# The up projection of a feed-forward layer: additions queued per part as the last passes are issued, pair loads placed further ahead, prepared sums in a buffer of their own

## The chip, the core and the metric

The kernel runs on one core of a Trainium2 chip. The metric is device time in microseconds (us) of one execution, median of several runs. TensorE does the matrix products (PE in the profile), VectorE (DVE) and ScalarE (ACT) prepare operands and move results, GpSimd (POOL) and SyncE (SP) here mostly issue transfers.

## What is computed

One decoder layer on 256 tokens of width 2048, all in float32: an RMSNorm, a joint input projection, two attention branches of 8 heads each, an output projection with residual, and a feed-forward part. The change is in the feed-forward part alone:

```python
h = _rmsnorm(x, norm_mlp_pre[layer])
u = jnp.square(jax.nn.relu(h @ w_up[layer]))      # w_up: 2048 x 8192
x = x + _rmsnorm(u @ w_down[layer], norm_mlp_post[layer])
```

## The kernel before

**Products.** Every float32 operand is split in two parts, `hi` (the rounded value) and `lo` (the remainder), and a product is three matmuls: hi\*hi, lo\*hi, hi\*lo. A weight tile is 128 rows x 1024 columns. ScalarE makes its `hi` (L306; L310 where a gain is multiplied in), then VectorE its `lo` (L307, L311). There are 8 buffers for split tiles (`W_BUFS`), so a split can be at most 8 tiles ahead of TensorE, and the program queues the splits 6 tiles ahead (`W_AHEAD`). Raw weights come through 5 `raw` buffers, loaded from SyncE's queue.

**Chunks.** `h @ w_up` is done in 8 chunks (`j`) of 1024 columns over 16 row blocks. The result of a chunk has four parts `(b, n)`: two halves of the tokens, two halves of the columns, each one PSUM bank (`acc`). The table `UP_STEPS` gives the steps of a chunk. `k8` is one row block: 12 matmuls. `w1` is a pair of row blocks (2 and 3) done with seven block products where eight would be needed (21 matmuls, four weight tiles): both raw blocks are loaded into the one buffer `ab` from GpSimd's queue (`load_two`), VectorE forms their sums `t` and `u` (L359, L363, L364; 2.6 us together in the trace), and four tiles are split: b11, b, u, t. `p0` is such a pair whose sums were made in DRAM earlier in the kernel (`prepare`), by transfers that add; its four tiles are loaded through `raw` buffers from SyncE's queue. Chunks 1 to 5 have the steps `k8 k9 k10 k11 p0 k12 w1 k13 w2 p3 k14 k15`, chunks 6 and 7 have three `w` pairs and no `p`.

**End of a chunk.** The seven products need four more PSUM banks (`m`). After a chunk's last pair, `close` turns them into four tiles `c` (L1052 on ScalarE, four L1055 on VectorE). Each part of the chunk is then finished by `up_evac`: VectorE adds `c` to the part (L954), ScalarE applies Relu (`r`, L957), TensorE transposes the result (`rt`, four small matmuls, L300), ScalarE squares it into `uT` (L971). These `rt` steps stand in TensorE's queue among the matmuls of the next chunk.

**Order.** Every engine takes its instructions in the order in which the program queued them. That order comes from `Flow`, a planning clock that advances by an assumed cost for every matmul; `up_evac` is a generator whose `yield` values say how long after one step the next is queued. In the kernel before, all four `up_evac` chains start at the end of the chunk, each with a delay of `UP_STEP * (o + 0.1)` ahead of its addition, `UP_STEP` = 2.2. `weights.first[i]` holds work that is queued just ahead of tile number `i`; `plan_seven` puts the sums of a `w` pair two tiles (`SUMS_AHEAD`) ahead of its first tile.

Tiles are numbered through the whole program. Chunk 1 begins with tile 137, chunk 2 with 161, chunk 3 with 185, chunk 4 with 209, chunk 5 with 233, chunk 6 with 257, chunk 7 with 279; the down projection `u @ w_down` begins with tile 301.

Of the kernel before, what the change touches and what calls it, by code (L numbers as in the profile page):

```python
# [18 lines left out]
F32 = mybir.dt.float32  # L19
# [4 lines left out]
OP = mybir.AluOpType  # L24
PSUM = bass.MemoryType.PSUM

P = 128
# [18 lines left out]
CW = 1024  # L46
# [46 lines left out]
D_UP, UP_STEP = 1.8, 2.2  # L93


SUMS_AHEAD = 2
NUP = FF // CW


def steps_of(text):  # L100

    return [(s[0], int(s[1:])) for s in text.split()]


UP_STEPS = {0: [("k", k) for k in range(KD)]}
for _j in range(1, 6):
    UP_STEPS[_j] = steps_of("k8 k9 k10 k11 p0 k12 w1 k13 w2 p3 k14 k15")
for _j in range(6, NUP):
    UP_STEPS[_j] = steps_of("k6 k7 k8 k9 k10 w0 k11 k12 w1 k13 w2 k14 k15")
SCALED = {j: range(8) for j in range(1, NUP)}  # L110
# [56 lines left out]
class Weights:  # L167
# [15 lines left out]
    def load(self, src, w, name, queue=None):  # L183
        raw = self.pool.tile([P, CW], F32, tag="raw", bufs=RAW_BUFS, name=name)
        out = raw[:, :w]
        if len(src.shape) == 3:
            out = out.rearrange("p (k n) -> p k n", k=src.shape[1])
        (queue or self.nc.sync).dma_start(out=out, in_=src)
        return raw
# [74 lines left out]
def layer(nc, tc, io):  # L264
    flow = Flow()
# [37 lines left out]
    def split(hi, lo, src, g=None):  # L303
        if g is not None:
            return split_gain(hi, lo, src, g)
        nc.scalar.activation(hi, src, AF.Copy)  # L306
        nc.vector.tensor_tensor(out=lo, in0=src, in1=hi.bitcast(F32), op=OP.subtract)  # L307
# [9 lines left out]
    weights = Weights(nc, wp, split, W_BUFS, W_AHEAD)  # L317
# [23 lines left out]
    def up_weight(j, k):  # L341
        return io["w_up"][k * P:(k + 1) * P, j * CW:(j + 1) * CW]

    late = {}
    sums_kept = {jk: dram.tile([P, 2 * CW], F32, name=f"sums{jk[0]}_{jk[1]}") for jk in PREP}

    def seven(load, targets):

        st, tt, H = {}, nc.vector.tensor_tensor, 512

        def sums():
            ab = load()
            a, b = st["a"], st["b"] = [ab[:, :CW], ab[:, CW:]] if not isinstance(ab, list) else ab
            t, u = st["t"], st["u"] = targets()
            if not isinstance(ab, list):
                two = [x.rearrange("p (k n) -> p k n", n=H) for x in (t, ab)]
                tt(out=two[0], in0=two[1][:, 0:2, :], in1=two[1][:, 1:4:2, :], op=OP.add)  # L359
            else:  # L360
                for x, o in ((a, 0), (b, H)):
                    tt(out=t[:, o:o + H], in0=a[:, o:o + H], in1=x[:, H:], op=OP.add)
            tt(out=u[:, :H], in0=t[:, :H], in1=b[:, H:], op=OP.add)  # L363
            tt(out=u[:, H:], in0=u[:, :H], in1=b[:, :H], op=OP.add)  # L364

        def b11(hi, lo):
            split(hi[:, :H], lo[:, :H], st["a"][:, :H])

        return sums, [b11] + [lambda hi, lo, n=n: split(hi, lo, st[n]) for n in "but"]

    def load_two(raw, queue, src):
        for i in range(2):
# [29 lines left out]
        st, left[c, kp] = down_parts(c, kp)  # L402
        nc.gpsimd.dma_start(out=st.bitcast(F32), in_=skeep[kp])

    def plan_seven(sums, fs, after, more=(), last=()):

        at = max(len(weights.specs) - SUMS_AHEAD, after)
        for n, f in (*more, (0, sums), *((0, f) for f in last)):
            weights.first.setdefault(at - n, []).append(f)
        return [weights.plan(f) for f in fs], len(weights.specs)  # L410

    wide_u, after = [], 0
    for j in range(NUP):
        wide_u.append([])
        for what, k in UP_STEPS[j]:
            if what == "k":
                g = () if k in SCALED.get(j, ()) else (gcol[:, 8 + k:9 + k],)
                ts = [weights.plan(up_weight(j, k), 1, CW, *g)]  # L420
            elif what == "p":
                kept = sums_kept[j, k]
                ts = [weights.plan(src, 1, n) for src, n in (
                    (up_weight(j, 2 * k)[:, :512], 512), (up_weight(j, 2 * k + 1), CW),
                    (kept[:, CW:], CW), (kept[:, :CW], CW))]
            else:
                ts, after = plan_seven(*seven_up(j, k), after)
            wide_u[j].append((what, k, ts))

    def down_weight(c, k):  # L430
# [518 lines left out]

    def up_evac(j, b, i, acc, order, more=None):  # L950

        yield UP_STEP * order
        if more is not None:
            nc.vector.tensor_tensor(out=acc, in0=acc, in1=more, op=OP.add)  # L954
            yield 1.6
        r = late["up"].tile([P, 512], F32, tag="r", bufs=2, name=f"r{j}_{b}")
        nc.scalar.activation(r, acc, AF.Relu, scale=rstd2[b])  # L957
        yield D_UP if j > 1 else 2 * D_UP
        t = bank(i, f"rt{j}_{b}")
        for k in range(4):  # L960
            transpose(t[:, k * P:(k + 1) * P], r[:, k * P:(k + 1) * P])
        if j not in uT:
            if j in (12, 13):
                t2 = late["ab"][:, (j - 12) * CW:(j - 11) * CW]
            elif j == 10:
                t2 = late["up"].tile([P, CW], F32, tag="uT10", bufs=1, name="uT10")
            else:
                tag = {"tag": "T", "bufs": 2} if j > 13 else {}
                t2 = late["up"].tile([P, CW], F32, name=f"uT{j}", **tag)
            uT[j] = t2.rearrange("p (k s) -> p k s", k=4)  # L970
        nc.scalar.activation(uT[j][:, :, b * P:(b + 1) * P], t.rearrange("p (k s) -> p k s", k=4), AF.Square)  # L971
# [53 lines left out]
    def some_sums(kps, after=0.0):  # L1025
        yield after
        for kp in kps:
            yield from left_sums(kp)
# [34 lines left out]
    for j in range(FF // CW):  # L1063
        at = {bn: 4 * (j % 2) + i for i, bn in enumerate(PARTS)}
        if j == 0:
            accs = {bn: acc_bank(f"acc_u0_{bn[0]}{bn[1]}") for bn in at}
            at = {bn: (turn[0] - 3 + i) % 4 for i, bn in enumerate(at)}
        else:
            accs = {bn: bank(i, f"acc_u{j}_{bn[0]}{bn[1]}") for bn, i in at.items()}
        steps = wide_u[j]  # L1070
        order = in_order(len(steps), (APART[1], 0)) if j == 0 else [(t, b) for t, (w, _, _) in enumerate(steps)
                                                                    for b in range(NB if w == "k" else 1)]
        for t, b in order:
            what, k, tiles = steps[t]
            if (j, t, b) == (0, 8, 0):
                flow.finish(*res)
                late["po"].release()
                mix.release()
                late["up"] = pool("up", "right")
                late["st"] = late["up"].tile([P, 3 * CW], F32R, tag="st", bufs=1, name="st")  # L1080
                for n in ("ab", "c"):
                    late[n] = late["up"].tile([P, 2 * CW], F32, name=n)
                late["st2"] = late["up"].tile([P, CW], F32R, tag="uT10", bufs=1, name="st2")
                flow.start(some_sums((0, 1)))
                flow.start(some_sums((2, 3), 18.0))
            if (j, t, b) == (FF // CW - 1, 4, 0):
                weights.limit -= 1
                u_next = split_u(0, 0)
            if what != "k":
                flow.until(lambda: len(sums) > k)  # L1090
            if what == "k":
                w = weights.get(tiles[0])
                h_done(k, b)
                for n in range(2):
                    c = slice(n * 512, (n + 1) * 512)
                    three(accs[b, n], [tok(hT[x], k, b) for x in range(2)], [w[x][:, 0, c] for x in range(2)], t == 0, t == len(steps) - 1)
                    if j == 0 and t == len(steps) - 1:
                        evac.append(flow.start(up_evac(n, b, at[b, n], accs[b, n], 2 * b + n - 0.25 * (2 * b + n))))
                    flow.pump()
                if b == NB - 1:  # L1100
                    weights.free(tiles[0])
                continue

            pairs = [s[1] for s in steps if s[0] != "k"]
            first, last = k == pairs[0], k == pairs[-1]
            if first:
                m = {n: bank(i, f"m{n}_{j}") for n, i in zip((1, 6, 7, 5), free)}
            blocks = [[tok(hT[x], 2 * k + kk, bb) for x in range(2)] for kk, bb in ((0, 0), (1, 0), (1, 1))]
            seven_products(tiles, (blocks, sums[k]), accs, m, first, last)
            if last:  # L1110
                more = close(closing(), m)
        free = [at[bn] for bn in PARTS]
        if j:
            for o, (b, n) in enumerate(PARTS):
                evac.append(flow.start(up_evac(2 * j + n, b, at[b, n], accs[b, n], o + 0.1, more[b, n])))
    u_last = evac[-4:]
    up = late["up"]

# [195 lines left out]
```

## Time and profile before

| | |
|---|---|
| median of 3 runs | 1063.76 us (1063.56 to 1064.2) |
| the profiled execution: its own time | 1066.42 us |
| its span from first to last instruction | 1064.6 us |
| PE busy | 1041.5 us (98%) |
| DVE busy | 811.2 us (76%) |
| ACT busy | 631.1 us (59%) |
| POOL busy | 94.5 us (9%) |
| mean granted TensorE clock | 0.997 |

In the trace chunk 1 begins at 403 us and the down projection at 719.5 us. A row of the timeline has the start, the time from start to end, engine, line, operation, what it writes and reads, the count of merged instructions, and in brackets the idle time ahead of it with what ended it. Matmuls overlap: one is shown 0.39 us long, and the next starts 0.227 us after it.

### The profile page before, as it was taken

The numbers are of one execution on the slowest core, as the hardware profiler recorded it, in microseconds if no ns is written. First come the engines' busy times: TensorE is split into PE (matmuls) and PEld (weight loads), VectorE is DVE, ScalarE is ACT, GpSimd is POOL, SyncE is SP. The second block draws the span as 40 slices with busy tenths as digits, with TensorE's granted clock in tenths as the row PEclk, the third lists the DMA queues.
The fourth block names the chain that finished last, engine by engine and source line by source line (L and its number), as shares of the span: only waits on it lengthen the run. The fifth ranks groups of instructions, "written<-read, shape, count | busy, mean of one in ns | idle before, by whom it ended". The sixth has DMA issues, their size and how long they took to land.

```text
span 1064.6 us, 13618 instructions
## 1 busy us (share of the span) xinstructions
PE 1041.5 (98%) x4839; PEld 863.4 (81%) x4839; DVE 811.2 (76%) x1083; ACT 631.1 (59%) x846; POOL 94.5 (9%) x148
## 2 busy tenths in 40 slices
PE   9999999999999999999999999999999999999996
PEld 6888899888888788777878778888888888888885
DVE  6666546577556678878788798988799978989995
ACT  6574436566454566565665657666566664766761
POOL 0011111112001000000000000001000001122100
PEclk9999999999999999999999999999999999999998
DMA  9999879699887285748676484469688867788952
GB/s 309 350 297 289 212 200 328 201 268 278 236 230 235 95 310 188 254 155 283 201 229 223 160 286 166 157 221 325 233 296 280 279 239 250 283 302 294 372 202 81
DMA packets 94724, 260.81 MB, mean 245 GB/s; under 512 B 8896, under 2 KB 13504, under 8 KB 94272
## 3 DMA queue, kind: packets, MB, share of 16 engines
q1 hardware_dynamic: 74080, 199.00, 54.3%
q0 software_dynamic: 20000, 60.30, 21.0%
q8 instruction: 38, 0.62, 0.2%
q10 hardware_dynamic: 576, 0.64, 0.2%
q14 instruction: 30, 0.25, 0.1%
HBM read 244.18 MB, written 39.32 MB: 266 GB/s over the span
## 4 chain that ended last, share of the span: by engine, by line
PE 72%; DVE 12%; DMA 8%; issue 4%; ACT 3%; DVEq 0%; POOL 0%; POOLq 0%; ACTq 0%; SPq 0%
PE y L296 25%; PE acc_o L296 8%; PE acc_u L296 6%; PE md L296 5%; PE acc_qk L296 4%; DVE lo L307 4%; PE acc_v L296 4%; DMA raw<-in_w_up 4%; PE acc_ckv L296 2%; DVE lo L311 2%; DMA ab<-in_w_up 2%; PE acc_ukv L296 2%; PE acc_q L296 2%; PE acc_cq L296 2%; PE acc_k L296 2%
## 5 line engine op out<-in xcount | busy, mean ns | idle before, releaser
L307 DVE TENSOR_TENSOR lo<-raw,hi 128x1024 fp32r<-128x1024 f32 (+3 forms) x257 | 288.0, 1142 | 96.5 <-ACT hi L306 95.8
L306 ACT ACTIVATE hi<-raw 128x1024 fp32r<-128x1024 f32 (+3 forms) x257 | 250.8, 992 | 101.4 <-PE y L296 20.8
L296 PE MATMUL y<-hi,uhi 128*128 128x512 f32 x376 | 146.6, 390 | 0.0
L296 PE MATMUL y<-hi,ulo 128*128 128x512 f32 x376 | 146.4, 389 | 0.0
L296 PE MATMUL y<-lo,uhi 128*128 128x512 f32 x376 | 146.3, 389 | 0.0
L296 PE MATMUL acc_u<-hi,hT_hi 128*128 128x512 f32 x356 | 142.4, 400 | 3.6 <-DVE c L1055 3.5
L296 PE MATMUL acc_u<-lo,hT_hi 128*128 128x512 f32 x356 | 139.1, 391 | 0.8 <-DVE lo L311 0.8
L296 PE MATMUL acc_u<-hi,hT_lo 128*128 128x512 f32 x356 | 139.2, 391 | 0.4 <-DVE hT_lo L307 0.4
L311 DVE SCALAR_TENSOR_TENSOR lo<-raw,gcol,hi 128x1024 fp32r<-128x1024 f32 x72 | 91.8, 1281 | 27.1 <-ACT hi L310 26.6
L310 ACT ACTIVATE hi<-raw,gcol 128x1024 fp32r<-128x1024 f32 x72 | 82.5, 1149 | 32.8 <-DMA raw<-in_w_up 18.3
L296 PEld LDWEIGHTS y<-lo,uhi 128*128 128x128 f32 x376 | 70.6, 188 | 14.7
L296 PEld LDWEIGHTS y<-hi,ulo 128*128 128x128 f32 x376 | 70.6, 188 | 14.6
L296 PEld LDWEIGHTS y<-hi,uhi 128*128 128x128 f32 x376 | 70.6, 188 | 14.5
L296 PEld LDWEIGHTS acc_u<-hi,hT_hi 128*128 128x128 f32 x356 | 66.9, 188 | 18.8 <-DVE c L1055 6.2
L296 PEld LDWEIGHTS acc_u<-hi,hT_lo 128*128 128x128 f32 x356 | 66.8, 188 | 15.1 <-DVE hT_lo L307 0.8
L296 PEld LDWEIGHTS acc_u<-lo,hT_hi 128*128 128x128 f32 x356 | 67.0, 188 | 14.0 <-DVE lo L311 1.2
L296 PE MATMUL m<-hi,st 128*128 128x512 f32 x156 | 56.5, 389 | 0.0
L296 PE MATMUL acc_o<-hi,mixT_hi 128*128 128x512 f32 x128 | 51.8, 405 | 0.0
L307 DVE TENSOR_TENSOR lo<-st_down,hi 128x1024 fp32r<-128x1024 f32 x40 | 48.0, 1220 | 4.0 <-ACT hi L306 3.8
L296 PE MATMUL acc_o<-hi,mixT_lo 128*128 128x512 f32 x128 | 50.2, 392 | 0.0
L296 PE MATMUL acc_o<-lo,mixT_hi 128*128 128x512 f32 x128 | 50.0, 390 | 0.0
L306 ACT ACTIVATE hi<-st_down 128x1024 fp32r<-128x1024 f32 x40 | 42.1, 1052 | 11.1 <-PE y L296 9.5
(326 smaller groups left out, 2000.8 us busy)
## 6 DMA issues: line engine op xcount, KB each, us to landing
raw<-in_w_down SPq DMA_DIRECT2D x88, 512.0 KB, 5.9
raw<-in_w_up SPq DMA_DIRECT2D x86, 512.0 KB, 5.0
raw<-in_w_in SPq DMA_DIRECT2D x55, 512.0 KB, 6.2
raw<-in_w_out SPq DMA_DIRECT2D x32, 512.0 KB, 7.5
ab<-in_w_up POOLq DMA_DIRECT2D x28, 512.0 KB, 4.9
sums<-in_w_up SPq DMA_DIRECT2D x20, 512.0 KB, 7.2
raw<-sums SPq DMA_DIRECT2D x20, 512.0 KB, 3.9
ab_down<-in_w_down POOLq DMA_DIRECT2D x20, 512.0 KB, 6.7
```

What stands on the lines that cost most here:

```text
L296: nc.tensor.matmul(out, a, b, start=start, stop=stop)
L306: nc.scalar.activation(hi, src, AF.Copy)
L307: nc.vector.tensor_tensor(out=lo, in0=src, in1=hi.bitcast(F32), op=OP.subtract)
L310: nc.scalar.activation(hi, src, AF.Copy, scale=g)
L311: nc.vector.scalar_tensor_tensor(out=lo, in0=src, scalar=g, in1=hi.bitcast(F32), op0=OP.mult, op1=OP.subtract)
```

## The change

1. `up_evac` is started for each part right after the part's last matmuls are issued, and queues the addition 0.2 us later by the planning clock. Relu follows 1.4 us and then `UP_STEP * 0.75 * (2b + n)` later.
2. The load of a `w` pair (`early`) is queued up to `LOAD_AHEAD` = 3 tiles ahead of its sums, in chunks 1 to 6 and for the first pair of chunk 7.
3. In chunks 1 to 4 the prepared sums (t and u of a `p` pair) come in one load of 1 MB into the buffer `tu`, from GpSimd's queue; before, they were two loads of 512 KB through `raw` buffers from SyncE's queue. Chunk 5 keeps the old way.
4. In chunks 1 to 5 the pairs 2 and 3 change roles: `p2` stands between `w1` and `w3`, so the last pair is now `w3`.
5. `uT` tiles 8 and 9 take the place of `tu` once it is no longer needed.

```diff
-SUMS_AHEAD = 2
+SUMS_AHEAD, LOAD_AHEAD = 2, 3
 for _j in range(1, 6):
-    UP_STEPS[_j] = steps_of("k8 k9 k10 k11 p0 k12 w1 k13 w2 p3 k14 k15")
+    UP_STEPS[_j] = steps_of("k8 k9 k10 k11 p0 k12 w1 k13 p2 w3 k14 k15")
...
         def sums():
-            ab = load()
+            ab = st["ab"] if "ab" in st else load()
...
-        return sums, [b11] + [lambda hi, lo, n=n: split(hi, lo, st[n]) for n in "but"]
+        def early():
+            st["ab"] = load()
+
+        return sums, [b11] + [lambda hi, lo, n=n: split(hi, lo, st[n]) for n in "but"], early
...
-    def plan_seven(sums, fs, after, more=(), last=()):
+    def plan_seven(sums, fs, early, after, more=(), last=(), soon=False):
 
         at = max(len(weights.specs) - SUMS_AHEAD, after)
+        if soon:
+            more = (*more, (at - max(at - LOAD_AHEAD, after - 2), early))
...
-                ts = [weights.plan(src, 1, n) for src, n in (
-                    (up_weight(j, 2 * k)[:, :512], 512), (up_weight(j, 2 * k + 1), CW),
-                    (kept[:, CW:], CW), (kept[:, :CW], CW))]
+                srcs = [(up_weight(j, 2 * k)[:, :512], 512), (up_weight(j, 2 * k + 1), CW),
+                        (kept[:, CW:], CW), (kept[:, :CW], CW)]
+                if j < 5:
+                    at = max(len(weights.specs) - 2 * LOAD_AHEAD, after_p)
+                    weights.first.setdefault(at, []).append(
+                        lambda kept=kept: nc.gpsimd.dma_start(out=late["tu"], in_=kept))
+                    ts = [weights.plan(src, 1, n) for src, n in srcs[:2]] + [weights.plan(
+                        lambda hi, lo, o=o: split(hi, lo, late["tu"][:, o:o + CW])) for o in (CW, 0)]
+                    after_p = len(weights.specs)
+                else:
+                    ts = [weights.plan(src, 1, n) for src, n in srcs]
             else:
-                ts, after = plan_seven(*seven_up(j, k), after)
+                ts, after = plan_seven(*seven_up(j, k), after, soon=j < NUP - 1 or k == 0)
...
     def up_evac(j, b, i, acc, order, more=None):
 
+        if more is not None:
+            yield 0.2
+            nc.vector.tensor_tensor(out=acc, in0=acc, in1=more, op=OP.add)
+            yield 1.4
         yield UP_STEP * order
-        if more is not None:
-            nc.vector.tensor_tensor(out=acc, in0=acc, in1=more, op=OP.add)
-            yield 1.6
         r = late["up"].tile([P, 512], F32, tag="r", bufs=2, name=f"r{j}_{b}")
...
+            elif j in (8, 9):
+                if j == 8:
+                    late["uT8"] = late["up"].tile([P, 2 * CW], F32, tag="uT8", bufs=1, name="uT8")
+                t2 = late["uT8"][:, (j - 8) * CW:(j - 7) * CW]
...
+                late["tu"] = late["up"].tile([P, 2 * CW], F32, tag="uT8", bufs=1, name="tu")
...
-                    if j == 0 and t == len(steps) - 1:
-                        evac.append(flow.start(up_evac(n, b, at[b, n], accs[b, n], 2 * b + n - 0.25 * (2 * b + n))))
+                    if t == len(steps) - 1:
+                        evac.append(flow.start(up_evac(2 * j + n, b, at[b, n], accs[b, n], 0.75 * (2 * b + n),
+                                                       more[b, n] if j else None)))
...
-        if j:
-            for o, (b, n) in enumerate(PARTS):
-                evac.append(flow.start(up_evac(2 * j + n, b, at[b, n], accs[b, n], o + 0.1, more[b, n])))
```

VectorE's queue around the end of chunk 2, before. `c` is a tile of `close`, `lo189` a split of weight tile 189, `acc_u2_01` part (0, 1) of chunk 2, `t3_1` and `u3_1` the sums of pair `w1` of chunk 3:

```order
L1055 TENSOR_TENSOR c_3572<-c_3572,m7_2_4242 128x512
L307 TENSOR_TENSOR lo189_4467<-raw189_4464,hi189_4466 128x512
L307 TENSOR_TENSOR lo190_4485<-raw190_4482,hi190_4484 128x1024
L307 TENSOR_TENSOR lo191_4507<-raw191_4504,hi191_4506 128x1024
L954 TENSOR_TENSOR acc_u2_00_4127<-acc_u2_00_4127,c_3572 128x512
L359 TENSOR_TENSOR t3_1_4525<-ab_3571 128x1024
L363 TENSOR_TENSOR u3_1_4526<-t3_1_4525,ab_3571 128x512
L364 TENSOR_TENSOR u3_1_4526<-u3_1_4526,ab_3571 128x512
L307 TENSOR_TENSOR lo192_4533<-raw192_4530,hi192_4532 128x1024
L954 TENSOR_TENSOR acc_u2_01_4128<-acc_u2_01_4128,c_3572 128x512
L954 TENSOR_TENSOR acc_u2_10_4129<-acc_u2_10_4129,c_3572 128x512
L311 SCALAR_TENSOR_TENSOR lo193_4564<-raw193_4561,gcol_69,hi193_4563 128x1024
```

The same place now (L967 is the addition, L1073 the last operation of `close`):

```order
L1073 TENSOR_TENSOR c_3572<-c_3572,m7_2_4241 128x512
L307 TENSOR_TENSOR lo189_4459<-raw189_4456,hi189_4458 128x512
L307 TENSOR_TENSOR lo190_4477<-raw190_4474,hi190_4476 128x1024
L967 TENSOR_TENSOR acc_u2_00_4128<-acc_u2_00_4128,c_3572 128x512
L967 TENSOR_TENSOR acc_u2_01_4129<-acc_u2_01_4129,c_3572 128x512
L967 TENSOR_TENSOR acc_u2_10_4130<-acc_u2_10_4130,c_3572 128x512
L307 TENSOR_TENSOR lo191_4500<-tu_3574,hi191_4499 128x1024
L967 TENSOR_TENSOR acc_u2_11_4131<-acc_u2_11_4131,c_3572 128x512
L359 TENSOR_TENSOR t3_1_4527<-ab_3571 128x1024
L363 TENSOR_TENSOR u3_1_4528<-t3_1_4527,ab_3571 128x512
L364 TENSOR_TENSOR u3_1_4528<-u3_1_4528,ab_3571 128x512
L307 TENSOR_TENSOR lo192_4533<-tu_3574,hi192_4532 128x1024
```

The first addition stands one split earlier, the other three stand ahead of the three sums, and `lo191`, `lo192` read `tu`.

TensorE's queue at the first transposes of chunk 2's result (`rt4_0`), before; tile 186 is the second tile of chunk 3:

```order
L296 MATMUL acc_u3_10_4502<-hi186_4425,hT_lo_2921 128x512
L296 MATMUL acc_u3_11_4503<-hi186_4425,hT_hi_2920 128x512
L296 MATMUL acc_u3_11_4503<-lo186_4426,hT_hi_2920 128x512
L296 MATMUL acc_u3_11_4503<-hi186_4425,hT_lo_2921 128x512
L300 MATMUL rt4_0_4553<-ident_94,r4_0_4539 128x128 x4
L296 MATMUL acc_u3_00_4500<-hi187_4437,hT_hi_2920 128x512
```

And now; tile 185 is the first tile of chunk 3:

```order
L296 MATMUL acc_u3_10_4497<-hi185_4406,hT_lo_2921 128x512
L296 MATMUL acc_u3_11_4498<-hi185_4406,hT_hi_2920 128x512
L296 MATMUL acc_u3_11_4498<-lo185_4407,hT_hi_2920 128x512
L296 MATMUL acc_u3_11_4498<-hi185_4406,hT_lo_2921 128x512
L300 MATMUL rt4_0_4518<-ident_94,r4_0_4507 128x128 x4
L296 MATMUL acc_u3_00_4495<-hi186_4415,hT_hi_2920 128x512
```

The transposes moved 12 matmuls earlier: they stand 12 matmuls into the next chunk, where before they stood 24 in. The other three of each chunk moved 12 earlier as well (21, 30 and 39 instead of 33, 42 and 51), and so at the ends of chunks 1 to 7; those of chunk 0 stay.

GpSimd's queue before, where it enters the up projection:

```order
L504 TENSOR_TENSOR rstd_pre20_3413<-t_pre20_3412,neg_half_92 128x1
L504 TENSOR_TENSOR rstd_pre21_3508<-t_pre21_3507,neg_half_92 128x1
L374 DMA ab_3571<-in_w_up 128x1024 x28
L374 DMA ab_down_6360<-in_w_down 128x1024 x2
L374 DMA c_3572<-in_w_down 128x1024 x2
```

And now:

```order
L517 TENSOR_TENSOR rstd_pre21_3508<-t_pre21_3507,neg_half_92 128x1
L433 DMA tu_3574<-sums1_0_70 128x2048
L377 DMA ab_3571<-in_w_up 128x1024 x2
L433 DMA tu_3574<-sums1_2_71 128x2048
L377 DMA ab_3571<-in_w_up 128x1024 x2
L433 DMA tu_3574<-sums2_0_72 128x2048
L377 DMA ab_3571<-in_w_up 128x1024 x2
```

Eight loads of `tu` now stand between the pair loads, in chunks 1 to 4.

More of the change, by code (lines that the diff above doesn't have):

```diff
@@ L410, in plan_seven @@
         return [weights.plan(f) for f in fs], len(weights.specs)
-    wide_u, after = [], 0
+    wide_u, after, after_p = [], 0, 0
     for j in range(NUP):
```

## The prediction

> **What bounds the kernel now.** I read the page's table of engines first, then busy time by stage, then what TensorE waits for, then the timelines around those waits.
>
> ```profile
> PE 1041.5 (98%) x4839; PEld 863.4 (81%) x4839; DVE 811.2 (76%) x1083; ACT 631.1 (59%) x846; POOL 94.5 (9%) x148
> 403.00:719.50 316.50, 304.33 (x1379) 247.03 (x1378) 263.36 (x286) 197.54 (x231) 13.97 (x26) 1.00 0.64 211
> 719.50:1047.00 327.50, 327.50 (x1454) 271.24 (x1453) 285.24 (x325) 201.65 (x224) 33.28 (x62) 1.00 0.78 272
> ```
>
> The stage rows give the length, then busy time of PE, weight loads, DVE, ACT, POOL, and the granted clock (1.00). TensorE is the bound: it is idle for 23.1 us of the 1064.6. Half of that, 12.2 us, lies in chunks 1 to 7 of the up projection (403 to 719.5); the down projection behind it has none. So the change can win only by taking TensorE's waits out of chunks 1 to 7. All of them there:
>
> ```profile
> PE rt L300 <- ACT r L957: 7.7, 6, 1.6
> PE acc_u L296 <- DVE c L1055: 3.5, 3, 1.3
> PE acc_u L296 <- DVE lo L311: 0.8, 1, 0.8
> ```
>
> Ten waits, 12.0 us: six of transposes on Relu (ends of chunks 1 to 4), three of a chunk's first matmuls on `close` (one when chunk 2 begins, two when chunk 6 begins), one on a late split (chunk 1). A wait costs more than is recorded for it. One that waited, and one that didn't:
>
> ```profile
> 457.03 0.40 PE L296 MATMUL acc_u<-hi,hT_lo 128*128 128x512 f32 x1
> 459.00 0.66 PE L300 MATMUL rt<-ident,r 128*128 128x128 f32 x4 [1.58 <-ACT r L957]
> 459.42 0.47 PE L296 MATMUL acc_u<-hi,hT_hi 128*128 128x512 f32 x1
> ...
> 463.95 0.40 PE L296 MATMUL m<-hi,hT_lo 128*128 128x512 f32 x1
> 464.19 0.60 PE L300 MATMUL rt<-ident,r 128*128 128x128 f32 x4
> 464.54 0.48 PE L296 MATMUL acc_u<-hi,hT_hi 128*128 128x512 f32 x1
> ```
>
> From matmul to matmul 2.39 us against 0.59: 1.80 lost where 1.58 is recorded, 0.22 more per wait. The ten cost 12.0 + 2.2 = 14.2 us, the most that the change can win.
>
> **Why the transposes wait: the end of chunk 2.** Chunk 3 begins at E = 493.91 (first row).
>
> ```profile
> 493.91 0.39 PE L296 MATMUL acc_u<-hi,hT_hi 128*128 128x512 f32 x1
> ...
> 499.69 0.60 PE L300 MATMUL rt<-ident,r 128*128 128x128 f32 x4
> ...
> 488.60 3.87 DVE L311 SCALAR_TENSOR_TENSOR lo<-raw,gcol,hi 128x1024 fp32r<-128x1024 f32 x3 [0.81 <-ACT hi L310]
> 492.39 2.28 DVE L1055 TENSOR_TENSOR c<-m,c 128x512 f32<-128x512 f32 x3
> 494.70 0.69 DVE L1055 TENSOR_TENSOR c<-c,m 128x512 f32<-128x512 f32 x1
> 495.30 2.95 DVE L307 TENSOR_TENSOR lo<-raw,hi 128x512 fp32r<-128x512 f32 x3
> 498.17 0.69 DVE L954 TENSOR_TENSOR acc_u<-acc_u,c 128x512 f32<-128x512 f32 x1
> 498.77 1.21 DVE L359 TENSOR_TENSOR t<-ab 128x1024 f32<-128x1024 f32 x1
> 501.36 1.22 DVE L307 TENSOR_TENSOR lo<-raw,hi 128x1024 fp32r<-128x1024 f32 x1
> 502.50 1.29 DVE L954 TENSOR_TENSOR acc_u<-acc_u,c 128x512 f32<-128x512 f32 x2
> ...
> 498.90 0.69 ACT L957 ACTIVATE r<-acc_u,rstd_pre 128x512 f32<-128x512 f32 x1 [0.50 <-DVE acc_u L954]
> 503.22 0.69 ACT L957 ACTIVATE r<-acc_u,rstd_pre 128x512 f32<-128x512 f32 x1 [3.63 <-DVE acc_u L954]
> ```
>
> The second addition stands behind three sums and a split, so it begins 4.3 us after the first; its Relu ends at 503.9, where the second transposes wait 1.6 us. The change takes those four operations away from in between. But it also moves all transposes 12 matmuls (12 x 0.227 = 2.72 us) earlier, so the first ones, which did not wait here, now have a deadline. From an addition's start to its transposes takes 499.69 - 498.17 = 1.52 us. The transposes now stand at E + 2.72; so the first addition must begin by E + 1.20.
>
> When can it begin? Ahead of it in VectorE's queue stand the four operations of `close` (492.39 to 495.30, 2.91 us) and now two splits instead of three (2.95 us for three, 1.74 for two). `close` needs the last pair's products, which end two steps before the chunk's end: 24 x 0.227 = 5.44 us. The earliest start is E - 5.44 + 2.91 + 1.74 = E - 0.8, which leaves 2.0 us of slack. Today VectorE comes to `close` at 492.39 = E - 1.5, 3.9 us after the earliest. If it stays that late, the first addition begins at 498.17 less one split (1.13) = 497.04 = E + 3.1, and TensorE waits 1.9 us. What decides is whether VectorE gets 1.9 us earlier per chunk.
>
> **What VectorE gains within a chunk.**
>
> ```profile
> DVE t L359 <- DMA ab<-in_w_up: 14.8, 6, 3.0
> ACT hi L306 <- DMA raw<-sums: 12.2, 8, 2.9
> POOL ab L374 <- DVE lo L307: 267.9, 25, 39.1
> ...
> 446.81 0.39 PE L296 MATMUL acc_u<-hi,hT_hi 128*128 128x512 f32 x1
> 421.04 1.22 DVE L307 TENSOR_TENSOR lo<-t,hi 128x1024 fp32r<-128x1024 f32 x1
> 425.25 1.23 DVE L359 TENSOR_TENSOR t<-ab 128x1024 f32<-128x1024 f32 x1 [3.00 <-DMA ab<-in_w_up]
> ```
>
> (a) *Order of the pairs.* Today `w2` follows `w1` with one tile between, and VectorE waits for `ab`: 14.8 us in six waits, 2.5 each, once in each of chunks 1 to 6. With `p2` between, VectorE has four 1024-column splits and one of 512 (some 5.3 us) between freeing `ab` and the sums, against a load of 4.8 us (row below). Five of the six waits go; chunk 6 keeps its own. Gain 2.5 us per chunk. (b) *Prepared sums in `tu`.* ScalarE's waits on `raw<-sums`, 12.2 us in chunks 1 to 5, mostly go: `tu` is free when the pair before has been split, half a chunk ahead, and the `raw` buffers turn over six times per pair section, not ten, so the six splits at the chunk's end find their weights loaded. Before the last three of them VectorE waits 0.8 us in chunk 2 (row 488.60). (c) *The load-ahead* by itself is worth nothing: GpSimd has nothing else to do there and stands waiting for the split that frees `ab` (267.9 us in 25 waits); the place of the load in the program only sets the turns with `tu`. (d) The additions themselves take no more time, 4 x 0.6 us.
>
> (a) alone is more than the 1.9 us needed, (b) comes on top, and VectorE's work (263 us in this stage, unchanged by the edit) fits the 304 us that TensorE needs. So at the ends of chunks 2, 3 and 4 I expect `close` at its earliest and no wait. Three places remain.
>
> *End of chunk 1.* The gain starts only at 422.2, where the last split before 425.25 ends (row 421.04). From there the new order is split k13 (1.2), p2's two raw splits (1.7), the sums as `ab` lands (425.25 to 427.85, as now), two `tu` splits (2.3), four of w3 (4.0): 434.1. Six more splits at 1.28, the last held until its `raw` buffer is loaded (freed 435.4, some 5.5 us to land, 1.2 on ScalarE), end at 443.4; `close` and two splits make it 448.1. The chunk's end, today at 446.8 (first PE row), comes 1.0 us earlier by the vanished wait on a split: E = 445.8, deadline 447.0. TensorE waits 1.1 us.
>
> *Ends of chunks 5 and 6.* Here VectorE is held by the 8 buffers of split tiles, not by loads. The end of chunk 6:
>
> ```profile
> 666.12 1.06 ACT L306 ACTIVATE hi<-raw 128x1024 fp32r<-128x1024 f32 x1 [1.61 <-PE acc_u L296]
> ...
> 669.55 1.22 DVE L359 TENSOR_TENSOR t<-ab 128x1024 f32<-128x1024 f32 x1
> 672.14 1.27 DVE L311 SCALAR_TENSOR_TENSOR lo<-raw,gcol,hi 128x1024 fp32r<-128x1024 f32 x1
> 676.25 1.28 DVE L311 SCALAR_TENSOR_TENSOR lo<-raw,gcol,hi 128x1024 fp32r<-128x1024 f32 x1
> 677.44 1.82 DVE L307 TENSOR_TENSOR lo<-ab,hi 128x512 fp32r<-128x512 f32 x2
> ...
> 681.56 0.60 PE L300 MATMUL rt<-ident,r 128*128 128x128 f32 x4
> ```
>
> ScalarE waits for TensorE to free a tile at 666.12, and the sums of the next `w0` stand ahead of `close`. E = 681.56 - 5.44 = 676.12. The addition moves ahead of one of the two splits begun at 677.44, so to 678.04 = E + 1.92, 0.72 us past the deadline. No wait today becomes one of 0.72. Chunk 5's end has the same rows in the same order, and once its loads are not late it gets the same 0.72 in place of today's two waits on `close`. At the end of chunk 7 the order has no sums and I find none.
>
> Sum: 14.2 removed; added 1.1 + 0.72 + 0.72, and 3 x 0.22, together 3.2. Net 11.0 us. The traced execution's span becomes 1064.6 - 11.0 = 1053.6; its own time was 1066.4, 2.7 above the median of the runs, so I take the sum off the median: 1063.8 - 11.0 = 1052.8 us.
>
> **Moved loads.** Eight 1 MB loads on GpSimd's queue replace sixteen of 512 KB on SyncE's. The bytes stay.
>
> ```profile
> raw<-in_w_up SPq DMA_DIRECT2D x65, 512.0 KB, 4.8
> ab<-in_w_up POOLq DMA_DIRECT2D x26, 512.0 KB, 4.8
> raw<-sums SPq DMA_DIRECT2D x18, 512.0 KB, 3.9
> xkeep<-x SPq DMA_DIRECT2D x2, 1024.0 KB, 4.9
> ```
>
> A `tu` load has no row. Its time is bounded by the 1 MB transfer (4.9 us) and by two 512 KB loads one after the other (9.6); I take 7. The one for the next chunk's `p0` can start when `p2` is split (430.1 in the working above) and is needed when ScalarE reaches it, about 447: 17 us. Hidden at either end, so it adds nothing to the sum. If it were late, ScalarE would stand at the `tu` split that is queued right ahead of the first Relu, and TensorE behind that.
>
> The Trainium skill speaks against this move: "SBUF — State Buffer", section "SBUF: two separate sides", says that GpSimd cannot write descriptors while VectorE runs an operation in its two-port mode, so that a transfer issued by GpSimd seems blocked, and it advises the SyncE or ScalarE queue. By that rule the load would grow, and the sum with it once the 17 us are used up. This trace shows no such hold: with VectorE busy for 83% of the stage, GpSimd's pair loads land in the same 4.8 us as SyncE's.
>
> **Rivals.** *Nothing left over*: splits at chunks 1, 5 and 6 come 0.7 to 1.1 us sooner than worked out. Against it, the buffer limit at 666.12. 1063.8 - 14.2 = 1049.6. Chance 0.12.
> *Half the gain*: VectorE gets about 1 us less than needed at the ends of chunks 2, 3 and 4, because 1 MB `tu` loads lie beside `ab` and `raw` loads and each lands later. Each boundary keeps about 1 + 0.22: 1052.8 + 3.7 = 1056.5. Chance 0.14.
> *No earlier at all*: the waits only trade places. 1.9 + 0.22 at four ends (8.5), the two waits on `close` at the start of chunk 6 stay (3.5 less some 1.2 for the one in chunk 2, and 2 x 0.22: 2.7), 0.94 after chunk 6: 12.1 of 14.2 remain, 1061.7, which is no clear change. Chance 0.08.
> *Slower: late `tu`.* Decides from a load of 17 us; beyond, each us costs a us at the three ends where a `tu` split is ahead of Relu (1, 2, 3), so 11.0 is lost at 17 + 3.7 = 21 us. At 24 us the time is 1052.8 + 21 = 1074. For it: GpSimd's queue is in order, and a held `tu` also holds the pair load behind it. Against: the 4.8 us rows. Chance 0.05.
>
> **How the numbers follow.** The forecast has 0.59, its own range 1050.5 to 1055; the cases above 0.39; 0.02 is unnamed. I take 1049 to 1058.5: it holds the forecast, "nothing left over" and "half the gain", and leaves out the last two. No change means within 0.2%, about 2.1 us, which is what runs of this kernel can tell apart. Faster: 0.59 + 0.12 + 0.14 and a little of the fourth, 0.87; same 0.07; slower 0.06.
>
> **What the profile after would show.** Right: TensorE's waits on Relu and `close` sum to about 2.5 us in three waits, at the first transposes of chunks 1, 5 and 6; VectorE's waits on `ab` fall from six to one; ScalarE's waits on sums from memory nearly vanish; `close` ends near E - 2.5 at chunks 2 to 4; the down projection has no idle time and begins 11 us earlier. Wrong: the first transposes wait at every chunk's end (VectorE not earlier), ScalarE waits on `tu`, or idle time turns up in the down projection.

## The result, and the profile after

The changed kernel takes 1052.57 us (median of 4 runs, 1051.04 to 1053.19) against 1063.98 for the kernel before on the same chip: ratio 0.989, 95% interval 0.9873 to 0.9907. The profiled execution took 1053.19 us, its span is 1051.4.

The engines' line of the page, and the busy time of two stages: chunks 1 to 7 of the up projection, and the down projection (columns as in the prediction).

```profile
PE 1038.0 (99%) x4839; PEld 864.5 (82%) x4839; DVE 811.1 (77%) x1083; ACT 633.6 (60%) x846; POOL 99.1 (9%) x156
403.14:706.33 303.19, 300.99 (x1380) 248.40 (x1378) 263.48 (x286) 200.17 (x232) 17.82 (x33) 1.00 0.64 216
706.33:1033.90 327.57, 327.57 (x1454) 271.27 (x1453) 285.15 (x325) 201.87 (x224) 33.40 (x62) 1.00 0.77 273
```

Before, the same seven chunks took 316.56 us (402.96 to 719.52). They lost 13.4 us; ahead of them and behind them the two traces differ by 0.2 us at most. VectorE's work is the same. TensorE's idle time there fell from 12.2 us to 2.2, and its busy time by 3.4 us as well, which the section on the reasons comes back to.

The waits in chunks 1 to 7 (engine, line, what was waited for: us, times, longest):

```profile
DVE t L359 <- DMA ab<-in_w_up: 3.0, 2, 2.8
ACT hi L306 <- DMA raw<-sums: 2.5, 1, 2.5
PE rt L300 <- ACT r L971: 2.2, 3, 1.2
```

VectorE's waits on `ab` fell from 14.8 us to 3.0, ScalarE's on prepared sums from 12.2 to 2.5, and of TensorE's ten waits three new ones are left. The end of chunk 2, which the prediction showed with a wait of 1.58 us (TensorE's and VectorE's timelines; chunk 3 begins at E = 489.93):

```profile
489.93 0.39 PE L296 MATMUL acc_u<-hi,hT_hi 128*128 128x512 f32 x1
...
492.66 0.60 PE L300 MATMUL rt<-ident,r 128*128 128x128 f32 x4
...
484.96 2.27 DVE L1073 TENSOR_TENSOR c<-m,c 128x512 f32<-128x512 f32 x3
487.27 0.69 DVE L1073 TENSOR_TENSOR c<-c,m 128x512 f32<-128x512 f32 x1
487.88 1.82 DVE L307 TENSOR_TENSOR lo<-raw,hi 128x512 fp32r<-128x512 f32 x2
489.62 1.89 DVE L967 TENSOR_TENSOR acc_u<-acc_u,c 128x512 f32<-128x512 f32 x3
```

`close` begins at E - 4.97 (before: E - 1.52) and ends at E - 1.97, where the prediction had some E - 2.5; the first addition begins at E - 0.31, and the transposes at E + 2.73 find their input ready. Chunks 3 and 4 end in the same way. The three waits, at the ends of chunks 1, 5 and 6, each at the first transposes, and what led to the second of them (chunk 6 begins at E = 618.07):

```profile
449.89 0.66 PE L300 MATMUL rt<-ident,r 128*128 128x128 f32 x4 [1.16 <-ACT r L971]
621.47 0.66 PE L300 MATMUL rt<-ident,r 128*128 128x128 f32 x4 [0.52 <-ACT r L971]
665.59 0.66 PE L300 MATMUL rt<-ident,r 128*128 128x128 f32 x4 [0.52 <-ACT r L971]
...
618.07 0.39 PE L296 MATMUL acc_u<-hi,hT_hi 128*128 128x512 f32 x1
...
620.00 1.89 DVE L967 TENSOR_TENSOR acc_u<-acc_u,c 128x512 f32<-128x512 f32 x3
```

The additions begin at E + 1.93, where the prediction had E + 1.92 and a deadline of E + 1.20.

### The profile page after: what moved, and what is told of

It is laid out like the page before. It is cut to its first block, busy times and chain, and to the rows that moved or that the text cites. A ratio compares the mean times of both kernels' runs of the same rounds, so it can differ in the third digit from the quotient of the medians.

```text
span 1051.4 us, 13574 instructions
## 1 busy us (share of the span) xinstructions
PE 1038.0 (99%) x4839; PEld 864.5 (82%) x4839; DVE 811.1 (77%) x1083; ACT 633.6 (60%) x846; POOL 99.1 (9%) x156
## 4 chain that ended last, share of the span: by engine, by line
PE 94%; DVE 2%; DMA 1%; issue 1%; ACT 1%; POOL 0%; DVEq 0%; POOLq 0%; ACTq 0%
PE y L296 26%; PE acc_u L296 23%; PE acc_o L296 8%; PE m L296 7%; PE md L296 5%; PE acc_qk L296 4%; PE acc_v L296 4%; PE acc_cq L296 2%; PE acc_ukv L296 2%; PE acc_q L296 2%; PE acc_k L296 2%; PE acc_uq L296 2%; PE rt L300 1%; PE acc_ckv L296 1%; DMA raw<-in_w_in 1%
## 5 line engine op out<-in xcount | busy, mean ns | idle before, releaser
L307 DVE TENSOR_TENSOR lo<-raw,hi 128x1024 fp32r<-128x1024 f32 (+3 forms) x241 | 269.9, 1137 | 97.7 <-ACT hi L306 97.0
L306 ACT ACTIVATE hi<-raw 128x1024 fp32r<-128x1024 f32 (+3 forms) x241 | 234.9, 988 | 99.6 <-PE y L296 21.4
L296 PEld LDWEIGHTS y<-hi,ulo 128*128 128x128 f32 x376 | 70.6, 188 | 14.8
L306 ACT ACTIVATE hi<-st_down 128x1024 fp32r<-128x1024 f32 x40 | 42.1, 1053 | 10.8 <-PE y L296 9.4
```

What stands on the lines that cost most here:

```text
L296: nc.tensor.matmul(out, a, b, start=start, stop=stop)
```

## Experiments

The change has three parts that can be made one without the other: the order of pairs, the buffer `tu`, the early additions with their transposes. The fourth, the load-ahead, needed no run: in the new order the program without it has the same instructions in the same order on every engine and queue. In the old order with `tu` it does set the turns of `ab` and `tu` on GpSimd's queue, so "`tu`" in the table stands for both together there. All times stand as ratios to the kernel before on the same chip, since its median was 1063.98 to 1066.14 us there; 0.001 is 1.06 us. The stage is chunks 1 to 7 in the profiled execution.

| order | `tu` | additions | ratio (95% interval) | stage, us |
|---|---|---|---|---|
| old | no | late (before) | 1 | 316.56 |
| old | no | early | 0.9949 (0.9933 to 0.9965) | 312.16 |
| old | yes | late | 1.0054 (1.0035 to 1.0074) | 322.10 |
| old | yes | early | 1.0035 (1.0018 to 1.0051) | 322.30 |
| new | no | late | 0.9857 (0.9834 to 0.9879) | 300.43 |
| new | no | early | 0.9862 (0.9847 to 0.9877) | 301.82 |
| new | yes | late | 0.9868 (0.9850 to 0.9885) | 302.06 |
| new | yes | early (the change) | 0.9890 (0.9873 to 0.9907) | 303.19 |

**Early additions alone.** The last two hunks of the change and the new `up_evac`; `UP_STEPS`, loads and buffers as before.

> Only the additions and transposes move; pair order, tu and load-ahead stay as in the kernel before. My theory: what pays is VectorE coming earlier to the chunk's end, and here it does not. With the start of close as it was (E - 0.28, - 1.52, - 1.55, - 1.42, + 1.05, - 2.78 for chunks 1 to 6) the first transposes now wait about 3 us at chunk 1, 1.9 at chunks 2, 3 and 4, up to 4 at chunk 5, 0.5 at chunk 6, in place of the waits on second transposes and some of those on close: 1061 to 1063, no clear change. Rival (the additions queued together bring the gain): about 1053, like the changed kernel.

Measured 0.9949: between the two, some 5 us faster where I had expected 1 to 3. TensorE's waits in the stage:

```profile
PE rt L300 <- ACT r L958: 5.3, 5, 1.5
PE acc_u L296 <- DVE c L1056: 3.1, 3, 1.4
PE acc_u L296 <- DVE lo L311: 0.6, 1, 0.6
```

Waits trade places, as the theory says (first transposes at five ends, 5.3 us), but cost less than worked out: at the ends of chunks 2 and 3 `close` began at E - 2.72 and E - 3.09 instead of E - 1.52 and E - 1.55. I had held VectorE's place against E fixed; but the time that TensorE waits at one end is time that VectorE gains on the next. This is argued and not tested; at the end of chunk 4 `close` began later than before (E - 0.95 instead of E - 1.42). Which of the freed waits carries the rest of the difference stays open.

**Additions late again in the changed kernel.** The reverse: all of the change but these hunks.

> The changed kernel with the additions and transposes where the kernel before has them (the first addition once the next chunk has begun, the other three behind the sums; first transposes at E + 5.44). My theory: VectorE comes to close 3.5 us earlier, so the second addition starts near E + 5.3, and its transposes at E + 8.2 need it by E + 6.6; no wait at chunks 2 to 6, about 0.7 at chunk 1; and the first transposes have 2.7 us more than in the changed kernel. 1050 to 1051, that is 2 us faster than the changed kernel. Rival (the second additions still come too late behind the sums, so queueing them together is needed): a wait of 1 us or more at each chunk's end remains, 1056 or more.

Measured 0.9868, one wait left, at the end of chunk 1:

```profile
401.70:703.76 302.06, 300.68 (x1380) 248.42 (x1379) 262.69 (x286) 198.79 (x232) 17.75 (x33) 1.00 0.64 217
PE rt L300 <- ACT r L970: 1.4, 1, 1.4
```

The second additions behind the sums are in time once VectorE is early. The rival is out: the early additions are not needed. The gain over the change (1.1 us in the stage) is less than the interval of the ratios can tell.

**The changed kernel without `tu`.**

```diff
-                if j < 5:
+                if j < 0:
```

> The changed kernel, but the prepared sums are loaded into the raw buffers as before (no tu loads); pair order, load-ahead and early additions stay. My theory by the prediction's term (a): the waits on ab (2.5 us per chunk) go with the order alone and that is more than the 1.9 needed: close at E - 4 or so at chunks 2 to 4, 1052.5 to 1054. ScalarE's waits on sums from memory stay near 12 us. Rival (the buffer tu is needed): about half the gain, 1056 to 1059.

Measured 0.9862, at least as fast as with `tu`. Waits of ScalarE and VectorE in the stage:

```profile
ACT hi L306 <- DMA raw<-sums: 6.2, 5, 1.7
DVE t L359 <- DMA ab<-in_w_up: 2.2, 1, 2.2
```

The waits on prepared sums, which `tu` was to remove, fell by half here without it (12.2 to 6.2).

**The old order in the changed kernel, and `tu` alone.**

```diff
-    UP_STEPS[_j] = steps_of("k8 k9 k10 k11 p0 k12 w1 k13 p2 w3 k14 k15")
+    UP_STEPS[_j] = steps_of("k8 k9 k10 k11 p0 k12 w1 k13 w2 p3 k14 k15")
```

> The changed kernel with the old order of pairs (w2 before p3); tu, load-ahead and early additions stay. My theory: the six waits on ab of about 2.5 us stay, so VectorE gets only what the missing waits on prepared sums give, at most 2.4 us per chunk and less where the two waits overlap; first additions come near the deadline or 1 us late: 1054 to 1058. Rival A (tu alone does it all): 1053. Rival B (tu is worth nothing): 1061 to 1062.

Measured 1.0035, slower than before: neither theory nor rival. What `tu` does there, with the additions late (the kernel before with `tu` and the load-ahead alone):

> The kernel before with tu and load-ahead alone: old order of pairs, additions and transposes where they were. My theory: in the old order a tu load waits for the pair's split with the two ab loads behind it on GpSimd's queue, and then all three go out at once, beside weight loads that land in 10 us instead of 4.6; the last weight before close comes late, VectorE 3 to 5 us late at the chunk's end. So it is slower than before by about as much as tu cost with the early additions (10 us there): ratio 1.004 to 1.010. Rival (the harm came from the early transposes' deadline, which is 2.7 us later here): 0.998 to 1.002.

Measured 1.0054, in the expected range. GpSimd's queue and ScalarE at the end of chunk 1, the loads issued in that stretch (KB, us from issue to landing), and, as the last row, ScalarE in the kernel before:

```profile
438.47 0.54 POOL L433 DMA_DIRECT2D tu<-sums  x1 [16.74 <-DVE lo L307]
439.00 1.07 POOL L377 DMA_DIRECT2D ab<-in_w_up  x2
...
447.79 1.15 ACT L310 ACTIVATE hi<-raw,gcol 128x1024 fp32r<-128x1024 f32 x1 [5.71 <-DMA raw<-in_w_up]
...
raw<-in_w_up SPq DMA_DIRECT2D x6, 512.0 KB, 9.3
tu<-sums POOLq DMA_DIRECT2D x1, 1024.0 KB, 9.0
ab<-in_w_up POOLq DMA_DIRECT2D x2, 512.0 KB, 11.5
```

```profile
439.04 6.26 ACT L310 ACTIVATE hi<-raw,gcol 128x1024 fp32r<-128x1024 f32 x5 [4.57 <-DMA raw<-in_w_up]
```

The `tu` load waits for the pair's split, both `ab` loads stand behind it, and when it goes all three go. The weight loads beside them take 9.3 us instead of the 5.5 of the same stretch in the kernel before, and the last weight ahead of `close` keeps ScalarE waiting for 5.7 us; `close` begins at E + 0.70. In the kernel before ScalarE waits at an earlier weight (4.57 us) and then takes five in a row without a wait. In the changed kernel `tu` and `ab` go out close together too, but nearly 8 us earlier in the chunk, ahead of the run of weights at its end, and the weight loads around them take 5.0 us:

```profile
431.29 0.54 POOL L433 DMA_DIRECT2D tu<-sums  x1 [9.67 <-DVE lo L307]
...
431.89 0.54 POOL L377 DMA_DIRECT2D ab<-in_w_up  x1
...
raw<-in_w_up SPq DMA_DIRECT2D x7, 512.0 KB, 5.0
```

What TensorE loses in the stage of the kernel with `tu` alone is only in small part idle time. Its row:

```profile
402.56:724.66 322.10, 309.13 (x1379) 250.52 (x1378) 262.90 (x286) 197.25 (x232) 17.74 (x33) 0.98 0.59 203
```

Of the 5.5 us more than before, idle time is 0.8 (13.0 instead of 12.2) and busy time 4.7 (309.1 instead of 304.4). About 4.4 of these lie behind the ends of chunks 1, 2 and 5, where after two or three waits in a row on `close` 22 steps from matmul to matmul take 0.43 us instead of 0.227; the last section shows the first of these places.

To test the burst, the pair load was put ahead of `tu` on GpSimd's queue:

```diff
-            more = (*more, (at - max(at - LOAD_AHEAD, after - 2), early))
+            more = (*more, (at - max(at - (14 if after else LOAD_AHEAD), after - 2), early))
```

> As the kernel with tu alone, but on GpSimd's queue the pair load for the next chunk's w1 stands ahead of the tu load for its p0, so it goes out when w2 is split and not behind tu when p3 is split. Nothing else moves. My theory: tu costs time in the old order because tu and two ab loads go out together beside the last weights of the chunk, 4.66 MB in 13 us, with the DMA engines full. 1 MB less there is about 2.5 us less at 415 GB/s for the last weight before close, at the ends of chunks 1, 2, 3 and 5: ratio to before 0.997 to 1.001, against 1.0054. Rival (the burst is not what matters): 1.004 or more.

```profile
430.21 0.54 POOL L377 DMA_DIRECT2D ab<-in_w_up  x1 [8.97 <-DVE lo L307]
431.34 0.54 POOL L377 DMA_DIRECT2D ab<-in_w_up  x1 [0.60 <-DVE lo L307]
437.62 0.54 POOL L433 DMA_DIRECT2D tu<-sums  x1 [5.74 <-DVE lo L307]
...
raw<-in_w_up SPq DMA_DIRECT2D x6, 512.0 KB, 7.0
```

Measured 1.0015 (1.0006 to 1.0024), just above the range I gave: the order on one queue, with nothing else moved, gives back about 4 of the 5.7 us that `tu` alone costs, and the weight loads fall from 9.3 to 7.0 us. How it gives them back is shown only in part. The last weight before `close` comes 0.9 us earlier at the end of chunk 1, not 2.5, and ScalarE still waits 5.1 us for it. The stage is 3.5 us shorter than with `tu` alone, and most of that is the slow steps of 0.43 us: 8 are left of 22. Also, 1.3 of the 3.5 us lie behind the end of chunk 5, where no `tu` load stands in the queue. So the order on the queue is shown to matter; that the burst is what costs the time is shown for the 0.9 us at the end of chunk 1 and argued for the rest.

**The order alone.** One string of the kernel before:

```diff
-    UP_STEPS[_j] = steps_of("k8 k9 k10 k11 p0 k12 w1 k13 w2 p3 k14 k15")
+    UP_STEPS[_j] = steps_of("k8 k9 k10 k11 p0 k12 w1 k13 p2 w3 k14 k15")
```

> The kernel before with one edit: pair p2 stands between w1 and w3. No tu, no load-ahead, additions and transposes where they were. My theory: the order is the whole gain. As in the run of the changed kernel without tu, VectorE starts close near E - 3.4 at chunk 1 and E - 5.2 at chunks 2 to 4; the late transposes (E + 5.44) then leave no wait at any chunk's end. Chunks 1 to 7 take 300.4 to 301.0 us against 316.6: ratio to before 0.984 to 0.986, 2 to 4 us faster than the changed kernel. Rival (the order needs the early additions, since the second addition stands behind the sums): waits of 1 us or more at several ends, ratio 0.990 or more.

Measured 0.9857 (0.9834 to 0.9879). Stage row and VectorE's wait on `ab`:

```profile
402.62:703.05 300.43, 300.43 (x1379) 248.50 (x1378) 262.27 (x286) 198.71 (x231) 14.03 (x26) 1.00 0.67 221
DVE t L359 <- DMA ab<-in_w_up: 1.7, 1, 1.7
ACT hi L306 <- DMA raw<-sums: 7.9, 7, 2.4
```

TensorE is busy for all of the 300.43 us: nothing is left to win from waits in this stage. ScalarE still waits 7.9 us on prepared sums, so those waits are not on the path. The one string does at least as much as the whole change; in the traced stage it does 2.8 us more.

**Is it the wait on `ab`?** The order also moves other loads, so the wait was shortened in another way: in the kernel before, `ahead` 0 instead of 2 for `w2` of chunks 1 to 5, which puts its sums behind the split of k13.

```diff
-        at = max(len(weights.specs) - SUMS_AHEAD, after)
+        at = max(len(weights.specs) - ahead, after)
```

> The kernel before, but in chunks 1 to 5 VectorE's sums for w2 stand behind the split of k13 instead of ahead of it; the order of pairs, loads, additions and transposes stay. It covers 1.2 us of the 2.5 to 3 us that VectorE waits for ab. My theory (the wait on ab is what makes VectorE late, us for us): the waits on ab fall from 15 to about 9 us, VectorE comes 1.2 us earlier to each chunk's end, chunks 1 to 7 take 308 to 311 us instead of 316.6: ratio 0.992 to 0.995. Rival A (the order pays through the turns of the raw buffers, not through ab): 0.998 or more. Rival B (a little is enough, since the slack is shared): 0.988 or less.

```profile
402.42:713.10 310.68, 302.69 (x1379) 247.47 (x1378) 263.53 (x286) 197.69 (x231) 14.03 (x26) 1.00 0.65 214
DVE t L359 <- DMA ab<-in_w_up: 8.5, 6, 3.0
```

Ratio 0.9946 (0.9934 to 0.9959), stage 310.68 us, waits on `ab` 8.5 us: as expected. 6.3 us less waiting of VectorE gave 5.9 us of the stage; the order took away 13.1 and gave 16.1. ScalarE's waits on prepared sums hardly moved (12.2 to 10.8), and `close` begins 1.0 to 1.5 us earlier against E at the ends of chunks 2 to 5, as the 1.2 us that the edit covers ask for. The dose fits the wait on `ab` as the cause, and rival A is out.

**Transposes later in the changed kernel.**

```diff
-        yield D_UP if j > 1 else 2 * D_UP
+        yield D_UP + 1.4 if j > 1 else 2 * D_UP
```

> The changed kernel with its transposes 6 matmuls (1.36 us) later. My theory: the three waits that are left (1.16, 0.52 and 0.52 us, with the slow spacing behind each 2.8 us) are all of one kind, a first transpose on a first addition, so they all go, and nothing else becomes late: chunks 1 to 7 take 300.4 to 300.9 us against 303.2, ratio to before about 0.9865. Rival (the later transposes hold the banks, and the waits come back in the next chunk, or ScalarE falls behind): 303 us or more, ratio 0.989.

The first transposes of each chunk stand 6 matmuls later, the other three 9. Measured 0.9857 (0.9839 to 0.9876), stage 300.44 us and all of it busy: the three waits that were left are of one kind, as forecast, and they cost 2.8 us. VectorE waits 5.5 us on `ab` in this run and TensorE never: a wait of VectorE costs time only where it makes VectorE late at a chunk's end.

**`tu` on SyncE's queue.**

```diff
-                        lambda kept=kept: nc.gpsimd.dma_start(out=late["tu"], in_=kept))
+                        lambda kept=kept: nc.sync.dma_start(out=late["tu"], in_=kept))
```

> The changed kernel with its eight tu loads on SyncE's queue. The Trainium skill (SBUF - State Buffer, SBUF: two separate sides) would make the loads on GpSimd's queue late while VectorE runs in its two-port mode: by that the loads land over 1 us sooner here than the 5.1 us of the changed kernel, and nothing is lost. My theory: no such hold is seen, the load lands in 5.1 us give or take 0.5 on either queue; what changes is that SyncE's queue is in order, and its weight loads now stand behind a tu load that waits for a split: same time within 2 us at best, up to 8 us slower if the weight loads are held.

Measured 1.0332 (1.0311 to 1.0352). Landing times of the eight `tu` loads, first of the changed kernel, then of this one; then the waits of SyncE's queue and of ScalarE:

```profile
DMA to landing us min/median/max: 5.0/5.1/7.5
```

```profile
DMA to landing us min/median/max: 4.8/4.9/8.9
...
SPq L433 <- DVE lo L307: 123.7, 7, 21.0
ACT hi L310 <- DMA raw<-in_w_up: 51.3, 15, 8.7
```

The load itself is as fast on either queue. But SyncE's queue carries the weights, and it stood for 123.7 us ahead of seven `tu` loads, with the weight loads behind it. ScalarE then waited 51.3 us for weights. The size, some 47 us against the changed kernel, was far above the 8 us that I had given as the most.

## Why the prediction was right, and where it was not

The time is right (1052.8 forecast, 1052.57 measured) and the mechanism is: VectorE must come 1.9 us earlier to each chunk's end, and the waits on `ab` are where it gets them. Step by step:

- *Where VectorE gains, (a).* Right, and stronger than said: the order alone brings all of it. 2.5 us per chunk was the size; six waits on `ab` became two, not one, and the second is 0.2 us.
- *(b), the buffer `tu` "on top".* Wrong. In the new order it brings nothing (1.4 us lost in the stage, with early additions); in the old one it costs 5.7 us, with the load-ahead and the additions late. I counted the waits that it removes (they did go, 12.2 to 2.5), but they were not on the path: with the order alone 7.9 us of them are left, and TensorE does not wait. The rival "half the gain" named the mechanism, `tu` loads beside `ab` and `raw` loads; it acts in the old order, and most of the cost there is slowed matmuls, which no term of the sum had.
- *(c), the load-ahead.* Worth nothing in the new order, as said. It sets the turns with `tu`, as said too, and in the old order the turns are worth 4 us.
- *The early additions.* The prediction took the operations moved out of the way as a part of the cure, and the earlier transposes as its price. With VectorE early, the second additions are in time anyway, and only the price is left: the three waits, 2.8 us. In the old order they gain 5 us; the rival "no earlier at all" had 2.
- *The three waits.* 1.1 forecast and 1.16 measured at the end of chunk 1, whose working held in its steps (E forecast 445.8, measured 445.85). At chunks 5 and 6 the transposes came 0.68 us late (E + 3.40 instead of E + 2.72), of which 0.52 is recorded; forecast were 0.72, to which I added 0.22 for what is not recorded, though 0.72 was already the whole lateness.
- *What a wait costs.* This term was too small. I took 0.22 us above the recorded 12.0, from one place, 14.2 in all. Against the stage without waits, 300.43 us, the ten had cost 16.1: 12.2 idle and 4.0 of busy time (304.39 in the row below against 300.43). That is 0.40 for each of the ten; in the changed kernel it was 0.19 (300.99 against 300.43, three waits). About 0.9 of the 4.0 us lie at three places where no wait is listed: 1.5 us into chunks 3, 4 and 5, two steps from matmul to matmul take 0.37 to 0.50 and 0.34 us instead of 0.227. The other 3.1 us are 0.3 for each listed wait. So the stage lost 13.4 us where the sum said 11.0. Chunks 1 to 7 of the kernel before:

```profile
402.96:719.52 316.56, 304.39 (x1380) 247.07 (x1378) 263.42 (x286) 197.58 (x231) 13.97 (x26) 1.00 0.64 211
```

- *From the trace to the median.* The error just named was covered by another: the profiled execution of before was 2.4 us above its median on this chip, that of after 0.6 above its own. Against the medians 11.4 are left of the traces' 13.2. The sum came out right within 0.4 us by two errors of some 2 us that cancel.
- *The down projection* has no idle time and begins 13.2 us earlier, not 11.
- *The rule of the Trainium skill* in "SBUF — State Buffer", section "SBUF: two separate sides". The landing times, 5.1 us on GpSimd's queue and 4.9 on SyncE's, show no hold of GpSimd's loads while VectorE is busy for 87% of the stage. No run shows whether VectorE's operations here are in the two-port mode, so the rule itself is not tested. To follow its advice, with SyncE's queue, took the ratio from 0.989 to 1.033, for a reason that lies in the order of SyncE's queue and not in the port.

## What to carry to other kernels

When the bounding engine waits on a helper at a stage's end, look for the helper's own longest wait in the middle of the stage, and see whether moving independent work into it is enough; here one swapped pair gave the whole gain and the rest of the change gave a little back. A buffer that takes waits away from an engine with slack is worth nothing, and its load may cost: look at which loads stand behind it on its queue and what goes out at the same moment. Price a wait of TensorE from a stretch without waits, not from the recorded idle time.

## What the runs showed of the hardware

A wait can lower TensorE's granted clock. With `tu` on SyncE's queue, after a wait of 6.53 us the granted clock was 0.50 and matmuls followed at 0.43 us instead of 0.227 for the next 5 us (row of the stretch: the granted clock is the third number from the end):

```profile
476.73 1.11 PE L300 MATMUL rt<-ident,r 128*128 128x128 f32 x4 [6.53 <-ACT r L971]
...
479.35 0.63 PE L296 MATMUL acc_u<-lo,hT_hi 128*128 128x512 f32 x1
...
479.00:482.00 3.00, 3.00 (x9) 2.32 (x8) 1.23 (x1) 0.70 (x2) 0.54 (x1) 0.50 0.60 175
```

Short waits in a row can do the same: with `tu` alone, three waits within 5.3 us, with three matmuls between each two, left the matmuls 0.43 us apart, and the granted clock of the four microseconds at 0.68.

```profile
449.47 0.50 PE L296 MATMUL acc_u<-hi,hT_hi 128*128 128x512 f32 x1 [1.50 <-ACT c L1069]
...
450.91 0.50 PE L296 MATMUL acc_u<-hi,hT_hi 128*128 128x512 f32 x1 [0.46 <-DVE c L1072]
...
453.22 0.63 PE L296 MATMUL acc_u<-hi,hT_hi 128*128 128x512 f32 x1 [1.35 <-DVE c L1072]
453.65 0.63 PE L296 MATMUL acc_u<-lo,hT_hi 128*128 128x512 f32 x1
...
452.00:456.00 4.00, 2.78 (x7) 2.20 (x8) 3.97 (x6) 2.95 (x3) 0.00 (x0) 0.68 0.60 190
```

Nearly the same three waits, again with three matmuls between each two (1.18, 0.46 and 1.35 us), left the clock at 1.00 in the changed kernel with the old order:

```profile
448.42 0.50 PE L296 MATMUL acc_u<-hi,hT_hi 128*128 128x512 f32 x1 [1.18 <-ACT c L1070]
...
452.17 0.50 PE L296 MATMUL acc_u<-hi,hT_hi 128*128 128x512 f32 x1 [1.35 <-DVE c L1073]
...
452.00:456.00 4.00, 2.42 (x12) 1.77 (x13) 4.00 (x7) 1.95 (x4) 0.00 (x0) 1.00 0.57 169
```

What decides between the two no run shows. The single waits of 1.6 us in the kernel before left the clock at 1.00. The Trainium skill, "TensorE: Matmul & The Clock Gate", Part 1, states that the clock halves after an idle window of about 3.4 us; the first case agrees with it, the second shows the halving without an idle time of that length.
